# Hybrid SSD, attention and mixture-of-experts block: Silu and splits on VectorE, the expert pairs' steps in another order, the last pair in one piece, the final norm by tiles

## The chip, the cores and the metric

The kernel runs on one core of a Trainium2 chip. TensorE (PE, with its weight loads as PEld), VectorE (DVE), ScalarE (ACT) and GpSimd (POOL) work in parallel, each through its own instructions in order, and meet through semaphores; SyncE (SP) issues nearly all DMAs. The metric is device time in microseconds of one execution.

## The reference

One transformer layer over 256 tokens of width 1024, in fp32: a projection of the normed input to some 6,500 columns, a Mamba2 mixer (causal convolution over four taps, Silu, a scan over chunks), a sparse attention mixer, their gated sum, and a mixture of experts, here the part that the change touches most:

```
xbc = jax.nn.silu(xbc + conv_b)                      # after the convolution
yg = yg * lax.rsqrt(jnp.mean(yg * yg, axis=-1, keepdims=True) + NORM_EPS)   # per group of 512
...
for e in range(N_EXPERTS):                            # 32 experts, top 2 of 8 within one of 4 groups
    he = jax.nn.silu(t @ w_g[e]) * (t @ w_u[e])       # 1024 -> 256
    out = out + combine[:, e:e + 1] * (he @ w_d[e])   # 256 -> 1024
...
return _rmsnorm(h, final_g)
```

## The kernel before

**First part, to about 473 us.** Projections are computed from weights that stream through slots of 1 MB. Each fp32 operand is split into a high and a low part: `split` (L217) has ACT copy the high part to `wh` and another engine subtract it to give the low part `wl` (L231 on POOL for every fourth of a range of splits, otherwise on DVE through `tt`, L91). PE then does three products. The order of the instructions on each engine in this part is made by a scheduler from its own estimates of cost, so the source shows less than the order lists do. From 62 to 107 us PE projects queries and keys (`qk`), from 107 to 170 the rest of the convolution's input (`pj_xb`), and between these stand the convolution's taps (L498 and `stt`, L88), ACT's Tanh (L504) and `conv_silu` (two POOL products, L508 and L509), and the rotary work (`RQ`). From 170 to 300 follow `z` and the attention, from 300 to 403 the gates and the scan, whose four groups each square y on ACT (`y2`) and sum the squares over the group's partitions by matmuls with a matrix of ones (`ysq`), then the output projections to 455, and the router.

**Experts, 473 to 694 us, written in order by hand** (`manual_schedule`, after L1457). 16 pairs p0 to p15 of two experts. A pair's tokens are gathered by a matmul with a 0/1 matrix, `DT`, into XG (for two pairs at a time: an odd pair gathers for the next two, `more`), 64 places per expert pair, the first 64 rows for the usual case and the other 64 (`others`) for an expert with more than 32 tokens, under a branch. Banks B4 to B7 of PSUM are shared. The steps of class `Pair`:

- `where` and `placed`: transposes of the weighted matrix `DW` into B5; from it DVE makes `DT` and `hp`, and ACT the routing weight of each row (`ws`, L1574).
- `up`: 32 matmuls into B4, gate and up of both experts side by side, k by k. `act`: Tanh (ACT, L1608), two products per half (DVE) into hp. `turn`: transposes of hp (L1617), `turned`: DVE copy to hT (`rw`, L1620).
- `down`: matmuls into B6. `result`: B6 times the gate g2 (DVE), copy of the high part (ACT, L1641), low part (DVE) into Y; Yo is the same for the others. `scatter`: matmuls of DT with Y's two parts into four accumulators (`acc`) that hold the residual stream, done in the next pair behind its `up`.
- `release` gives a weight slot back; SP then issues the next load in `stream`: per pair g, u, g, u, d, d of 1 MB each, for the last pair in 2, 4 and 2 pieces. SP waits in order for a slot.
- `general` is a loop over experts with still more tokens, that does nothing here; its register `ra` is loaded at pair 15 (L1687).

**End.** At pair 15, up and down go expert by expert. Then the final gain FG is loaded from ACT's queue (L1795), ACT loads the table of Sqrt (L1796), and the norm squares the accumulators (ACT, one on DVE), takes one root for both tiles and scales (L1813 to L1820).

## Time and profile before

| | us |
|---|---|
| median of three runs (lowest, highest) | 714.25 (708.05, 716.08) |
| profiled execution | 716.01 |
| its span | 714.0 |
| PE, DVE, ACT, POOL busy | 644.5, 470.2, 319.1, 63.0 |
| mean granted clock of TensorE | 0.972 |

The span is what the profile shows from the first to the last event; the execution is 2.0 longer. Times in the rows are from the start of the span. An engine that is busy all through a stretch sets its length; where none is, the waits tell which one was late. Of the granted clock, 1.00 is 2.4 GHz and 0.50 is 1.2 GHz.

### The profile page before, as it was taken

What the parts mean: (1) busy time and instruction counts of PE and PEld (TensorE: products, weight loads), DVE (VectorE), ACT (ScalarE), POOL (GpSimd) and SP (SyncE); (2) the same over time, 40 slices, a digit from 0 to 9 for tenths busy, and PEclk for the clock granted to TensorE, in tenths of its full rate; (3) what the DMA queues carried; (4) which work ended last, traced back from release to release, by engine and by line L of the source; (5) the groups of instructions that cost most, each with busy time, mean ns of one, the idle gap of its engine ahead of it and who ended that gap; (6) DMA issues with size and microseconds to landing.
All of it is one profiled execution on the core that took longest, in us unless ns stands there. A gap on an engine that the chain in (4) does not pass through costs nothing. (4 is left out here: it accounts for less than half of the span.)

```text
span 714.0 us, 14367 instructions
## 1 busy us (share of the span) xinstructions
PE 644.5 (90%) x5712; PEld 505.7 (71%) x5713; DVE 470.2 (66%) x1122; ACT 319.1 (45%) x622; POOL 63.0 (9%) x98
## 2 busy tenths in 40 slices
PE   6999989698999999999999999978888898888863
PEld 5889879697768778888988998755454554554530
DVE  3556899995789878695987677475454444554524
ACT  4335865663377776446554445421231212322212
POOL 2001682433000000000000000000000000000000
PEclk8899999999999999999999999998999999999986
DMA  8997941459748767626559888349999999999902
GB/s 269 334 344 253 363 136 21 158 178 308 226 160 283 256 198 253 219 77 219 173 182 351 345 344 315 122 162 380 375 421 419 419 419 421 418 420 417 371 12 89
DMA packets 102916, 193.28 MB, mean 271 GB/s; under 512 B 7716, under 2 KB 84020, under 8 KB 91316
## 3 DMA queue, kind: packets, MB, share of 16 engines
q1 hardware_dynamic: 101700, 190.26, 74.0%
q10 hardware_dynamic: 1136, 1.89, 0.9%
q8 instruction: 57, 0.93, 0.5%
q14 instruction: 23, 0.19, 0.1%
HBM read 190.98 MB, written 1.16 MB: 269 GB/s over the span
## 5 line engine op out<-in xcount | busy, mean ns | idle before, releaser
L105 PE MATMUL moe<-g,XG 128*32 128x256 f32 (+1 forms) x560 | 74.3, 385 | 3.5 <-PEq L1589 2.0
L105 PE MATMUL moe<-u,XG 128*32 128x256 f32 (+1 forms) x560 | 74.3, 386 | 0.0
L105 PEld LDWEIGHTS moe<-g,XG 128*32 128x32 f32 (+1 forms) x560 | 41.4, 113 | 39.0 <-issue 19.6
L105 PE MATMUL moe<-d,rw 128*32 128x512 f32 (+1 forms) x280 | 39.3, 644 | 15.2 <-ACT XG L1505 10.6
L88 DVE SCALAR_TENSOR_TENSOR hp<-hp,moe 64x256 f32<-64x256 f32 x32 | 13.4, 419 | 59.3 <-ACT hp L1608 59.1
L1608 ACT ACTIVATE hp<-moe 64x256 f32<-64x256 f32 x32 | 12.1, 378 | 65.1 <-PEq L1589 45.0
L105 PE MATMUL pj_z<-HH,wh 128*128 128x256 f32 x128 | 36.6, 286 | 2.6 <-DVE BC L88 2.1
L1574 ACT ACTIVATE moe<-moe 64x256 f32<-64x256 f32 x32 | 11.4, 356 | 59.3 <-DVE hp L95 58.8
L105 PEld LDWEIGHTS moe<-u,XG 128*32 128x32 f32 (+1 forms) x560 | 36.8, 113 | 0.0
L105 PE MATMUL pj_z<-HH,wl 128*128 128x256 f32 x128 | 36.8, 288 | 0.0
L105 PE MATMUL pj_z<-HL,wh 128*128 128x256 f32 x128 | 36.1, 282 | 0.0
L105 PE MATMUL moe<-DT,HFh 128*128 128x256 f32 x128 | 30.7, 291 | 2.1 <-DVE DT L91 1.1
L105 PEld LDWEIGHTS moe<-d,rw 128*32 128x32 f32 (+1 forms) x280 | 8.5, 117 | 33.8 <-issue 15.2
L919 ACT ACTIVATE P<-P,mn 128x128 f32<-128x128 f32 (+1 forms) x64 | 28.5, 448 | 6.4 <-DVE mn L916 5.4
L105 PE MATMUL pj_xb<-HH,wh 128*128 128x256 f32 x96 | 27.0, 282 | 3.9 <-DVE XSb L88 3.9
L105 PE MATMUL moe<-DT,HFl 128*128 128x256 f32 x128 | 29.6, 282 | 0.2 <-DVE HFl L88 0.2
L105 PE MATMUL moe<-Y,DT 64*128 64x512 f32 x128 | 20.7, 433 | 8.7 <-PEq L1589 3.3
L105 PE MATMUL xa<-HH,wh 128*128 128x256 f32 x96 | 28.6, 300 | 0.0
L91 DVE TENSOR_TENSOR moe<-moe,DW 128x512 f32<-128x512 f32 x16 | 11.2, 700 | 25.6 <-PE moe L105 13.1
L105 PE MATMUL pj_xb<-HH,wl 128*128 128x256 f32 x96 | 27.0, 281 | 0.9 <-DVE wl L91 0.9
L105 PEld LDWEIGHTS pj_z<-HH,wh 128*128 128x128 f32 x128 | 24.1, 188 | 5.3 <-issue 3.8
L91 DVE TENSOR_TENSOR wl<-so,wh 128x1024 fp32r<-128x1024 f32 x16 | 19.5, 1223 | 11.9 <-PE pj_so L105 10.8
(474 smaller groups left out, 2092.8 us busy)
## 6 DMA issues: line engine op xcount, KB each, us to landing
g<-in_w_exp_gate_dram SPq DMA_DIRECT2D x30, 1024.0 KB
u<-in_w_exp_up_dram SPq DMA_DIRECT2D x30, 1024.0 KB, 11.4
d<-in_w_exp_down_dram SPq DMA_DIRECT2D x30, 1024.0 KB, 16.8
ad<-in_w_ada_dram SPq DMA_DIRECT2D x16, 1024.0 KB, 6.3
ada<-in_w_ada_dram SPq DMA_DIRECT2D x16, 512.0 KB, 7.9
z<-in_w_in_dram SPq DMA_DIRECT2D x8, 1024.0 KB, 6.7
so<-in_w_ssm_out_dram SPq DMA_DIRECT2D x8, 1024.0 KB
qk<-in_w_in_dram SPq DMA_DIRECT2D x8, 936.0 KB, 7.3
```

Source lines behind the costliest of these rows:

```text
L88: return V.scalar_tensor_tensor(o, a, s, b, op0=op0, op1=op1)
L91: return V.tensor_tensor(o, a, b, op=op)
L105: return PE.matmul(o, l, r, start=start, stop=stop)
L919: A.activation(o, o, AF.Exp, bias=mn[:, n:n + 1], scale=-1.0, accum_out=sm[:, n:n + 1])
L1574: A.activation(B5[h, s * 256:(s + 1) * 256], B5[h, s * 256:(s + 1) * 256], AF.Copy, accum_out=self.ws[h])
L1608: A.activation(th[g], B4[g, s * 256:(s + 1) * 256], AF.Tanh, scale=0.5)
```

## The change

- All splits subtract on DVE; `conv_silu` is one DVE operation, q (tn + 1), in place of two POOL products.
- The four squares tiles of a group are added on DVE (two additions), and one matmul sums over the partitions in place of four.
- For pair 0 the routing arithmetic that needs no gather goes ahead of the gather on DVE, ACT makes all eight pieces of XG, and `where` goes between k = 5 and k = 6 of `up`.
- Odd pairs with a gather behind them: the second half of the gather and its copies come ahead of the next pair's `placed`.
- All other pairs: the first 64 rows are activated, turned into B7 and copied alone (`turn_of`, `turned_of`), then down; the other rows are turned behind down, and `placed` and the 0/1 matrices come behind that.
- The last pair's weights come as g, g, u, u, d, d in two pieces each; it does up and down in one; pair 14's scatter is behind its up; FG is loaded from SP after pair 14; the Sqrt table is loaded before down; `ra` is loaded after pair 13; the last scatter multiplies fp32 by halves of 256 columns straight from B6 times g2 (`scatter_last`).
- The norm goes tile by tile: accumulator times gain first, root of each tile apart, then the scaling.

Core of the diff:

```
-    for e in (NE - 2, NE - 1):
-        stream.append((f"g{e}", ld_rows(w_exp_gate, e, 2)))
-        stream.append((f"u{e}", ld_rows(w_exp_up, e, 4)))
-        stream.append((f"d{e}", ld_rows(w_exp_down, e, 2)))
+    for n, w in (("g", w_exp_gate), ("u", w_exp_up), ("d", w_exp_down)):
+        for e in (NE - 2, NE - 1):
+            stream.append((f"{n}{e}", ld_rows(w, e, 2)))
...
-        if PS0 <= st["split"] < PS1 and st["split"] % PSN == PSR:
-            G.tensor_tensor(lv, src, hv.bitcast(F32), op=OP.subtract)
-        else:
-            tt(lv, src, hv.bitcast(F32), OP.subtract)
+        tt(lv, src, hv.bitcast(F32), OP.subtract)
...
-        G.tensor_tensor(tn, tn, q, op=OP.mult)
-        G.tensor_tensor(q, tn, q, op=OP.add)
+        stt(q, tn, 1.0, q, OP.add, OP.mult)
...
+            tt(y2[0], y2[0], y2[1], OP.add)
+            tt(y2[0][:, 0:256], y2[0][:, 0:256], y2[0][:, 256:512], OP.add)
+            yield
             yb = ps(4, f"ysq{g}")[32 * g:32 * g + 32, 0:256]
-            for jj in range(2):
-                for j in range(2):
-                    mm(yb, ones[:, 0:32], y2[jj][:, j * 256:(j + 1) * 256], jj == 0 and j == 0, jj == 1 and j == 1)
+            mm(yb, ones[:, 0:32], y2[0][:, 0:256], True, True)
             A.activation(rs[32 * g:32 * g + 32], yb, AF.Copy)
...
+    def xg_copy(c, bank, first=False):
         for j in range(2):
             k, o, b_ = 2 * c + j, XG[:, (2 * c + j) * 256:(2 * c + j + 1) * 256], bank[:, j * 256:(j + 1) * 256]
-            if c % 2:
+            if c % 2 and not first:
...
-    for l in range(2):
-        for c, bank in enumerate((B4, B5, B6, B7)):
-            gather(bank, named, c, 256, (l,))
-            if l:
-                xg_copy(c, bank)
-    release("XK")
-    code = const([128, 16], "code", I32)
-    stt(code, ch, 2.0, qv[:, :, 0], OP.mult, OP.add)
     gs_ = rt(2)
     oh1, oh2, m1, m2, e2 = rt(2, 8), rt(2, 8), rt(2), rt(2), rt(2)
     ts(oh1, rank, 0.0, OP.is_equal)
     V.tensor_reduce(m1, leg, axis=AX.X, op=OP.max)
     stt(leg, oh1, -BIG, leg, OP.mult, OP.add)
     V.tensor_reduce(m2, leg, axis=AX.X, op=OP.max)
+    tt(e2, m2, m1, OP.subtract)
     ts(oh2, rank, 1.0, OP.is_equal)
-    tt(e2, m2, m1, OP.subtract)
+    V.tensor_reduce(gs_, ge, axis=AX.X, op=OP.add)
+    for l in range(2):
+        for c, bank in enumerate((B4, B5, B6, B7)):
+            gather(bank, named, c, 256, (l,))
     A.activation(e2, e2, AF.Exp)
-    V.tensor_reduce(gs_, ge, axis=AX.X, op=OP.add)
+    for c, bank in enumerate((B4, B5, B6, B7)):
+        xg_copy(c, bank, True)
+    release("XK")
+    code = const([128, 16], "code", I32)
+    stt(code, ch, 2.0, qv[:, :, 0], OP.mult, OP.add)
...
+        def act(self, parts=(0, 1)):
 
             lo, hi = slice(0, 64), slice(64, 128)
-            for s, (g, u) in enumerate(((lo, hi), (hi, lo))):
-                A.activation(th[g], B4[g, s * 256:(s + 1) * 256], AF.Tanh, scale=0.5)
-            for s, (g, u) in enumerate(((lo, hi), (hi, lo))):
+            gu = ((lo, hi), (hi, lo))
+            if 0 in parts:
+                for s, (g, u) in enumerate(gu):
+                    A.activation(th[g], B4[g, s * 256:(s + 1) * 256], AF.Tanh, scale=0.5)
+            for s in parts:
+                g, u = gu[s]
                 b = B4[:, s * 256:(s + 1) * 256]
                 stt(hp[u], th[g], 1.0, b[g], OP.add, OP.mult)
...
+        def turn_of(self, s):
+
+            q = slice(64 - 64 * s, 128 - 64 * s)
+            for m in range(2):
+                PE.transpose(B7[:, s * 128 + m * 64:s * 128 + (m + 1) * 64], hp[q, m:256:2], ident[q, q])
+
+        def turned_of(self, s):
+            V.tensor_copy(hT[:, :, 64 - 64 * s:128 - 64 * s],
+                          B7[:, s * 128:(s + 1) * 128].rearrange("p (m r) -> p m r", m=2))
+
...
+        def scatter_last(self):
+            mark(f"x_scatter{self.p}")
+            for n in range(2):
+                tt(YT[:, n], B6[:, n * 256:(n + 1) * 256], g2[:, n * 256:(n + 1) * 256], OP.mult)
+            for n in range(2):
+                for i in range(2):
+                    for hh in range(2):
+                        q = slice(64 * hh, 64 * hh + 64)
+                        mm(acc[i, hh][:, n * 256:(n + 1) * 256], self.DT[0][q, i * 128:(i + 1) * 128], YT[q, n], False, n == 1)
 
...
         if p == 15:
-            general()
-        if p < 15:
+            general(ra)
+        if p:
             P.up()
         else:
-            for j in range(2):
-                P.up((j,))
+            P.up(range(6))
+            P.where()
+            P.up(range(6, 8))
         P.asked()
         P.up_others()
         if not p:
-            P.where()
             P.placed()
-        if p < 15:
-            release(*(f"{n}{e}" for e in P.es for n in "gu"))
-        P.act()
+        release(*(f"{n}{e}" for e in P.es for n in "gu"))
         if more:
+            P.act()
             weighted(P.q + 1)
-        if prev and p < 15:
             prev.scatter()
             prev.scatter_others()
-        if more:
             for c, bank in enumerate((B6, B7)):
                 gather(bank, named, c, 256)
                 xg_copy(c, bank)
-        if nxt:
             nxt.where()
-        P.turn()
-        P.turned()
-        if nxt:
+            P.turn()
+            P.turned()
+            for c, bank in enumerate((B6, B7), 2):
+                gather(bank, named, c, 256)
+                xg_copy(c, bank)
             nxt.placed()
-        if not P.a and P.q < 7:
-            onehots(P.q + 1)
+        else:
+            P.act((0,))
+            if prev:
+                prev.scatter()
+                prev.scatter_others()
+            if nxt:
+                nxt.where((0,))
+            P.turn_of(0)
+            P.turned_of(0)
+            if nxt:
+                nxt.where((1,))
+            P.act((1,))
+        if p == 15:
+            A.activation(wss[0][0:1, 0:1], th[64:65, 0:1], AF.Sqrt, scale=0.0, bias=epsc[0:1])
+        P.down()
+        if not more:
+            P.turn_of(1)
+            P.turned_of(1)
+            if nxt:
+                nxt.placed()
+            if not P.a and P.q < 7:
+                onehots(P.q + 1)
+        P.down_others()
+        release(*(f"d{e}" for e in P.es))
+        if p < 15:
+            P.result()
+            P.result_others()
         if not p:
             left()
             release("G1")
-        if more:
-            for c, bank in enumerate((B6, B7), 2):
-                gather(bank, named, c, 256)
-                xg_copy(c, bank)
-        if p < 15:
-            P.down()
-            P.down_others()
-            release(*(f"d{e}" for e in P.es))
-            P.result()
-            P.result_others()
-        else:
-            P.down_others()
-            P.result_others()
-            for j in range(2):
-                P.down((j,))
-            P.result()
+        if p == 13:
+            ra = nc.values_load(any_[0:1, 0:1], min_val=0, max_val=4)
         if p == 14:
-            P.scatter()
-            P.scatter_others()
-    FG = slot("FG")
-    A.dma_start(FG[:, 0:1024], dram(final_g, 0, [[0, 128], [1, 1024]]))
-    A.activation(wss[0][0:1, 0:1], hp[32:33, 0:1], AF.Sqrt, scale=0.0, bias=epsc[0:1])
-    pairs[15].scatter_others()
-    pairs[15].scatter()
+            FG = slot("FG")
+            SP.dma_start(FG[:, 0:1024], dram(final_g, 0, [[0, 128], [1, 1024]]))
+    P.result_others()
+    P.scatter_others()
+    P.scatter_last()
 
 
     mark("last")
     OU, SJ = slot("OU"), slot("SJ")
     OUv, SJv = (t.rearrange("p (t d) -> p t d", t=2) for t in (OU, SJ))
-    sf, vf, rf = carve(rw_[:, 256:264], (2, 2), (2,), (2,))
-    for i in range(2):
+    sf, vf, rf, rv, r_ = carve(rw_[:, 256:268], (2, 2), (2,), (2,), (2,), (2,))
+
+    def cs(h):
+        return slice(h * 512, (h + 1) * 512)
+
...
+    half_norm(0)
+    times_g(0, 1)
+    times_g(0, 0)
+    root(0)
+    half_norm(1)
+    times_g(1, 1)
+    newton(0)
+    times_g(1, 0)
+    root(1)
+    for h in range(2):
+        ts(OUv[:, 0, cs(h)], OUv[:, 0, cs(h)], rf[:, 0:1], OP.mult)
+    SP.dma_start(out[0, 0:128, :], OUv[:, 0])
+    newton(1)
+    A.activation(OUv[:, 1, cs(1)], OUv[:, 1, cs(1)], AF.Copy, scale=rf[:, 1:2])
+    ts(OUv[:, 1, cs(0)], OUv[:, 1, cs(0)], rf[:, 1:2], OP.mult)
+    SP.dma_start(out[0, 128:256, cs(0)], OUv[:, 1, cs(0)])
+    A.dma_start(out[0, 128:256, cs(1)], OUv[:, 1, cs(1)])
```

DVE's list in an odd pair that gathers (pair 1): DW is the weighted 0/1 matrix, `XG<-moe,GC` the copies of gathered rows, `rw<-moe` the copy of the turned activations, `DT<-moe` and `hp<-moe` are `placed`. Before:

```order
L91 TENSOR_TENSOR DW<-DT,comb 128x2x64
L91 TENSOR_TENSOR DW<-DT,cE 128x2x64
L96 TENSOR_SCALAR XG<-moe_5299,GC 128x256 x2
L1620 COPY rw<-moe_5296 128x256
L95 TENSOR_SCALAR DT<-moe_5297 128x256
L95 TENSOR_SCALAR hp<-moe_5297 128x256
L96 TENSOR_SCALAR XG<-moe_5299,GC 128x256 x2
L1589 UNCONDITIONAL_BRANCH
L91 TENSOR_TENSOR moe_5298<-moe_5298,DW 128x512
```

And now:

```order
L90 TENSOR_TENSOR DW<-DT,comb 128x2x64
L90 TENSOR_TENSOR DW<-DT,cE 128x2x64
L95 TENSOR_SCALAR XG<-moe_5283,GC 128x256 x2
L1618 COPY rw<-moe_5280 128x256
L95 TENSOR_SCALAR XG<-moe_5283,GC 128x256 x2
L94 TENSOR_SCALAR DT<-moe_5281 128x256
L94 TENSOR_SCALAR hp<-moe_5281 128x256
L1584 UNCONDITIONAL_BRANCH
L90 TENSOR_TENSOR moe_5282<-moe_5282,DW 128x512
```

The second pair of XG copies moved ahead of `placed`; on ACT its own XG copies moved the same way ahead of the sums of `ws`.

PE's list of pair 0, from the end of `up`'s branch to pair 1's first matmul: `DW` rows are `where`, `hp` rows the turns, the rows that end in `,rw 32x512` down. Before (the 16 are pair 0's own eight and pair 1's eight):

```order
L1589 UNCONDITIONAL_BRANCH
L105 MATMUL moe_5297<-ident,DW 64x128 x16
L1617 MATMUL moe_5296<-ident,hp 128x128 x2
L105 MATMUL moe_5298<-d_4716,rw 32x512 x2
L105 MATMUL moe_5298<-d_4718,rw 32x512 x2
L105 MATMUL moe_5298<-d_4716,rw 32x512 x2
L105 MATMUL moe_5298<-d_4718,rw 32x512 x2
```

And now, behind an `up` that already has pair 0's own eight `where` rows in it:

```order
L1584 UNCONDITIONAL_BRANCH
L104 MATMUL moe_5281<-ident,DW 64x128 x4
L1624 MATMUL moe_5283<-ident,hp 128x64 x2
L104 MATMUL moe_5281<-ident,DW 64x128 x4
L104 MATMUL moe_5282<-d_4700,rw 32x512 x2
L104 MATMUL moe_5282<-d_4702,rw 32x512 x2
L104 MATMUL moe_5282<-d_4700,rw 32x512 x2
L104 MATMUL moe_5282<-d_4702,rw 32x512 x2
L1624 MATMUL moe_5283<-ident,hp 128x64 x2
```

The turn is split in two, the first ahead of half of the next pair's `where`, the second behind down; pair 0's own `where` has left this place.

PE's end. `Y,DT` and `Yo,DT` rows are the last scatter, into the four accumulators; the branch above them ends the others' scatter. Before:

```order
L1656 UNCONDITIONAL_BRANCH x2
L105 MATMUL moe_5292<-Y,DT 128x512
L105 MATMUL moe_5293<-Y,DT 128x512
L105 MATMUL moe_5292<-Y,DT 128x512
L105 MATMUL moe_5293<-Y,DT 128x512
L105 MATMUL moe_5294<-Y,DT 128x512
L105 MATMUL moe_5295<-Y,DT 128x512
L105 MATMUL moe_5294<-Y,DT 128x512
L105 MATMUL moe_5295<-Y,DT 128x512
```

And now:

```order
L1674 UNCONDITIONAL_BRANCH x2
L104 MATMUL moe_5276<-Yo,DT 128x256
L104 MATMUL moe_5277<-Yo,DT 128x256
L104 MATMUL moe_5278<-Yo,DT 128x256
L104 MATMUL moe_5279<-Yo,DT 128x256
L104 MATMUL moe_5276<-Yo,DT 128x256
L104 MATMUL moe_5277<-Yo,DT 128x256
L104 MATMUL moe_5278<-Yo,DT 128x256
L104 MATMUL moe_5279<-Yo,DT 128x256
```

The scatter is eight matmuls of 256 columns from one fp32 tile in place of eight of 512 from Y's two parts, the accumulators' left halves first.

## Rows read from the trace of the kernel before

**Rows 1.** The page, its part 1 (busy time, share of the span and instructions of each engine) and of part 2 the mean busy share of the core's 16 DMA engines in forty equal slices of 17.85 us, in tenths.

```profile
PE 644.5 (90%) x5712; PEld 505.7 (71%) x5713; DVE 470.2 (66%) x1122; ACT 319.1 (45%) x622; POOL 63.0 (9%) x98
...
DMA  8997941459748767626559888349999999999902
```

**Rows 2.** The windows view by stage: from and to, length, then busy time and number of instructions of PE, PEld, DVE, ACT and POOL, the granted clock, the DMA share and GB/s. The stages are the projection of queries and keys, the second half of the convolution with the rotary work beside it, the scan, and the experts' loop from the second pair's loads on.

```profile
62.00:107.00 45.00, 42.50 (x216) 36.67 (x215) 38.59 (x68) 34.46 (x49) 30.98 (x18) 1.00 0.84 275
107.00:170.00 63.00, 53.68 (x445) 50.29 (x443) 57.49 (x86) 38.20 (x64) 23.51 (x14) 1.00 0.45 142
300.00:403.00 103.00, 103.00 (x865) 92.64 (x865) 83.48 (x153) 55.26 (x70) 0.16 (x2) 1.00 0.63 215
478.00:680.00 202.00, 173.48 (x1898) 106.06 (x1902) 99.70 (x249) 50.27 (x134) 0.00 (x0) 0.97 0.99 402
```

**Rows 3.** The waits view of PE from 62 to 172 us: the waiting group, what it waited for, us in total, times, the longest.

```profile
PE pj_xb L105 <- DVE XSb L88: 3.9, 2, 3.2
PE qkp L105 <- POOL wl L231: 2.4, 2, 1.8
```

**Rows 4.** The timeline of DVE: start, duration of all instructions of the row, engine, line, operation, out<-in, shapes, count, and in brackets the idle time before with what ended it.

```profile
70.83 1.13 DVE L91 TENSOR_TENSOR wl<-qk,wh 128x936 fp32r<-128x936 f32 x1
...
82.88 1.92 DVE L91 TENSOR_TENSOR wl<-qk,wh 128x936 fp32r<-128x936 f32 x1
...
110.73 0.68 DVE L91 TENSOR_TENSOR RQ<-RQ 128x512 f32<-128x512 f32 x1
```

**Rows 5.** The timeline of POOL, same columns.

```profile
83.89 2.07 POOL L509 TENSOR_TENSOR XSa<-cv,XSa 128x512 f32<-128x512 f32 x1
```

**Rows 6.** DVE's groups of one shape from 62 to 175 us: line, operation, out<-in, shape, count, then busy us in total, mean ns of one, and idle time before.

```profile
L91 DVE TENSOR_TENSOR wl<-qk,wh 128x936 fp32r<-128x936 f32 x12 | 18.0, 1514 | 5.9 <-ACT wh L229 5.9
...
L91 DVE TENSOR_TENSOR RQ<-QKV,cs 128x512 f32<-128x512 f32 x8 | 9.7, 1232 | 0.1
L91 DVE TENSOR_TENSOR wl<-z,wh 128x1024 fp32r<-128x1024 f32 x4 | 6.7, 1671 | 1.8 <-ACT wh L229 1.8
```

**Rows 7.** POOL's groups in the same stretch, same columns.

```profile
L231 POOL TENSOR_TENSOR wl<-qk,wh 128x936 fp32r<-128x936 f32 x4 | 8.8, 2200 | 63.7 <-ACT wh L229 63.7
L231 POOL TENSOR_TENSOR wl<-xb,wh 128x1024 fp32r<-128x1024 f32 x3 | 7.8, 2607 | 15.6 <-ACT wh L229 15.6
```

**Rows 8.** The timeline of PE in the scan, the row of one group's sum of squares.

```profile
304.59 1.91 PE L105 MATMUL ysq<-y,ones 128*32 128x256 f32 x8
```

**Rows 9.** The timeline of all engines in pair 0: the transposes that place its weights (`where`), the tanh, the down projection, pair 1's first up matmul.

```profile
478.38 1.28 PE L105 MATMUL moe<-ident,DW 128*64 128x128 f32 x16 [1.14 <-DVE DW L91]
...
481.63 0.75 ACT L1608 ACTIVATE hp<-moe 64x256 f32<-64x256 f32 x2
...
485.57 3.64 PE L105 MATMUL moe<-d,rw 128*32 128x512 f32 x16 [0.52 <-DVE rw L1620]
...
489.39 0.41 PE L105 MATMUL moe<-g,XG 128*32 128x256 f32 x2 [0.18 <-PEq L1589]
```

**Rows 10.** The timeline from the end of pair 9 to the start of pair 11: pair 9's down projection, pair 10's first up matmul, the scatter of pair 9's result, the turn, pair 10's down projection, pair 11's first up matmul.

```profile
619.92 1.92 PE L105 MATMUL moe<-d,rw 128*32 128x512 f32 x16 [1.47 <-ACT XG L1505]
...
622.02 0.41 PE L105 MATMUL moe<-g,XG 128*32 128x256 f32 x2 [0.18 <-PEq L1589]
...
626.39 1.20 PE L105 MATMUL moe<-Y,DT 64*128 64x512 f32 x8 [0.71 <-PEq L1589]
...
629.11 0.50 PE L1617 MATMUL moe<-ident,hp 128*128 128x128 f32 x2 [0.27 <-DVE hp L88]
...
630.13 1.92 PE L105 MATMUL moe<-d,rw 128*32 128x512 f32 x16 [0.52 <-DVE rw L1620]
...
632.23 0.41 PE L105 MATMUL moe<-g,XG 128*32 128x256 f32 x2 [0.18 <-PEq L1589]
```

**Rows 11.** The waits view over the whole span, one line.

```profile
PE moe L105 <- ACT XG L1505: 10.6, 7, 1.8
```

**Rows 12.** The windows view along the stream of expert weights, columns as in group 2.

```profile
488.00:492.00 4.00, 3.82 (x57) 1.93 (x53) 2.95 (x9) 0.60 (x1) 0.00 (x0) 0.85 0.71 272
508.00:512.00 4.00, 4.00 (x68) 1.98 (x64) 1.29 (x2) 0.28 (x1) 0.00 (x0) 1.00 0.71 256
640.00:660.00 20.00, 17.05 (x220) 10.35 (x216) 10.57 (x24) 5.09 (x14) 0.00 (x0) 1.00 1.01 418
668.00:670.00 2.00, 1.14 (x12) 0.42 (x16) 0.42 (x1) 0.80 (x2) 0.00 (x0) 1.00 0.98 319
678.00:680.00 2.00, 1.48 (x14) 0.54 (x18) 1.09 (x3) 0.43 (x2) 0.00 (x0) 1.00 0.27 109
686.00:688.00 2.00, 2.00 (x14) 0.92 (x12) 0.00 (x0) 0.00 (x0) 0.00 (x0) 0.50 0.00 0
```

**Rows 13.** The timeline of the last pair: its first up matmul, the tanh, the down projection, the start of the norm, the last scalings.

```profile
685.43 0.61 PE L105 MATMUL moe<-g,XG 128*32 128x256 f32 x1 [1.51 <-PEq L1687]
...
694.40 0.77 ACT L1608 ACTIVATE hp<-moe 64x256 f32<-64x256 f32 x2 [12.24 <-PEq L1589]
...
698.26 3.17 PE L105 MATMUL moe<-d,rw 128*32 128x512 f32 x16 [0.52 <-DVE rw L1620]
...
704.29 0.69 DVE L1809 COPY SJ<-moe 128x512 f32<-128x512 f32 x1 [0.63 <-PE moe L105]
...
707.88 2.72 DVE L88 SCALAR_TENSOR_TENSOR OU<-moe,rw,FG 128x512 f32<-128x512 f32 x4
```

More of the change, by code (lines that the diff above doesn't have):

```diff
@@ L34 @@
 WARM3 = 12
-PS0, PS1, PSN, PSR = 17, 44, 4, 1
 RATE_XB, RATE_ATTN, RATE_SSD = 1.15, 1.5, 1.35
@@ L1558, in __init__, with where @@
             self.DT, self.ws, self.last = DTs[p % 2], wss[p % 2], p == 15
-        def where(self):
+        def where(self, ss=(0, 1)):
             mark(f"x_where{self.p}")
-            for s in range(2):
+            for s in ss:
                 for i in range(2):
```

55 lines of the change are left out of this document (26 added, 29 removed).

## The prediction

> **What bounds the kernel now.** I read the page first. PE is busy for 644.5 of the 714.0 us, DVE for 470.2, POOL for 63.0, and the DMA slices stand at 9 from the 28th on [rows 1]. An average says little here, so I went on by stages [rows 2]. The profiled execution took 716.0 us (span 714.0 and 2.0 around it); that is 1.8 above the median 714.25 of three runs that lie 8 us apart. The sum is made against 716.0.
>
> Three stages matter. From 62 to 170 us PE idles 2.5 + 9.3 = 11.8 us (length less busy), while DVE is busy 38.6 of 45 and 57.5 of 63 [rows 2]; PE's longest waits there are for DVE (3.9) and for a POOL subtraction (2.4) [rows 3]. From 300 to 403 PE has no idle time at all: 103.0 of 103 [rows 2]. In the expert loop PE is busy 173.5 of 202 and the DMA share is 0.99 [rows 2], so two chains run side by side: PE with the engines that feed it, and the weight stream. The stream is done in the window 678 to 680 (share 0.27, so about 678.5) [rows 12], but pair 15 starts only at 685.43 [rows 13]. From the last byte to the end of the span pass 35.5 us in which nothing is loaded for the experts.
>
> **The change, part by part.**
>
> *Splits and Silu to DVE.* POOL loses 7 subtractions (means 2.20 and 2.61) [rows 7] and 24 Silu products; the one on the timeline took 2.07 [rows 5]. DVE gains 7 subtractions at 1.13 alone [rows 4], the 1024-wide ones at 1024/936 of that: 4 x 1.13 + 3 x 1.24 = 8.2 us; and 12 fused products over 128x512 from SBUF, for which the nearest row is 0.68 [rows 4]: 8.2. Together +16.4. Against it: DVE's own operations with two SBUF inputs are longer beside POOL. The subtraction at 82.88 took 1.92 with POOL at work, that at 70.83 took 1.13 [rows 4, 5]; the means are 1.51, 1.23 and 1.67 where alone they are 1.13, 0.68 and about 1.24 [rows 4, 6]. With the counts 12, 8 and 4 that is 4.6 + 4.4 + 1.7 = 10.7 us in these three groups; with the small groups I estimate 18. Net on DVE: about -2. PE gains more than that, since the wait for POOL (2.4) goes and Silu is no longer two POOL steps behind the taps. Bounds: -11.8 (all PE idle time) and +16.4 (no relief, all on the path). I take **-5**, near the wait for POOL plus the net relief, because most of the idle time also hangs on the order that the scheduler lays out anew.
>
> *Sum of squares.* Each of four groups has 8 records in 1.91 us on a PE without idle time [rows 8, 2]; two stay. 4 x 1.3 = 5.2 us go. DVE pays 0.68 + about 0.4 per group, in a stage where it is busy 83.5 of 103 [rows 2]; if it were late, PE would wait. Bounds 0 and -5.2; I take **-5**, for the matmul has other work queued before it.
>
> *First pair.* DVE's routing arithmetic is taken out of the way of the gather's results and ACT makes all XG pieces, so DW is ready before the up projection ends. Before: `where` at 478.38, tanh at 481.63, down at 485.57, pair 1 at 489.39, and down took 3.64 instead of 1.92 because the clock stood at half after the idle stretch [rows 9, 10]. By the same steps, tanh comes at about 479.7 and pair 1 at about 486.4: -3.0. Worst case 0: ACT's pace of 0.5 per k against up's 0.46 may hold up the projection.
>
> *Odd pairs.* The second gather and its copies now stand ahead of `placed`. PE waited 10.6 us in 7 pairs for the copy into XG before down, 1.47 of it at pair 9 [rows 10, 11]; ACT then has nothing between. 7 x 1.35 = -9.5 (bounds 0, -10.6).
>
> *Even pairs.* From the start of the scatter to the start of down pass 3.74 us (626.39 to 630.13) [rows 10]; with the first rows turned alone, down waits for two DVE operations less, about 0.9, at 0.25 more PE work after down: 7 x (0.85 - 0.25) = -4.2. The result comes later, but the next up (3.7) covers it.
>
> *Last pair.* Between pair 14's down and pair 15's up stand a wait for Y, the scatter and the 1.51 of a register load [rows 13]: 4.5 us that go behind the up or to pair 13. PE alone would start pair 15 at 685.4 - 3.0 - 9.5 - 4.2 - 4.5 = about 664.
>
> *The weight stream.* That is before the weights. The stream ends at 678.5; its holes at 488 and 508 (share 0.71 of 4 us each: 2.3 us) [rows 12] go with the earlier releases, larger pieces at the end bring back about 1.0 (319 GB/s against 418) [rows 12], pair 0's release is later by 0.6: 675.8. The two down tiles are the last 5.0 us of it (1.05 MB at 418 GB/s each), so u31's first half is there at about 669.3. **PE waits about 5 us, and the stream becomes the bound.** Before, PE's idle stretch ahead of pair 15 left the clock at half (0.50 at 686 to 688, the 1.2 GHz level) [rows 12], so I price pair 15's up between 3.7 at full and 6.9 at half clock, at 6: 675.3. Tanh, products, half turn and copy 2.65 (today 698.26 - 694.40 = 3.86 [rows 13] less 0.9 and less the 0.3 of a shorter copy): 678. Down 3 (today 3.17): 681. Result times gate and fp32 scatter without Y: 2.4. Norm: today 9.7 from 704.29 to the end [rows 13]; of which the four scalings are 2.72; by tiles I count 9.9, four multiplications and four scalings in place of the four, overlapped with the squares, so no gain. End at 692.9 in the time of before: **-21.1** for experts and end together (bounds -28, if the clock holds and the stream ends a pair's piece earlier, and -14, if up and down run at half clock throughout and the holes stay).
>
> **Sum:** 716.0 - 5 - 5 - 21.1 = 684.9. I predict **685**. I don't take off the 1.8 to the median, as the three runs spread by more.
>
> **The page against the rows.** Pair 0's down, after idle time, took 3.64 against 1.92, and pair 15's up ran at 0.50 [rows 9, 10, 12]. The Trainium skill ("TensorE: Matmul & The Clock Gate", section "HAM oscillation — how this bites in real kernels") says that a kernel whose matmuls are shorter than its wait for weights has every tile start at the throttled clock. That speaks against a change which makes PE faster than its stream; it would give about 692 in place of 685. Rows show it only after the two long idle stretches, and in between the granted clock is 1.00 [rows 2, 12].
>
> **Rivals.**
>
> 1. *The front gives nothing.* DVE stays at its limit from 62 to 170 since the added 16.4 eats the relief, and the sum of squares waits for DVE. For it: DVE at 57.5 of 63 [rows 2]. Against: the stretch beside POOL is measured. Time: 685 + 5 + 5 = 695.
> 2. *More of the front, warm end.* All idle time of 62 to 170 goes (-11.8 in place of -5) and pair 15 runs at full clock (-2.3 on up): 676. For it: PE's work from 62 on is dense; against: pair 15 must wait for weights.
> 3. *Half clock whenever PE has caught up.* PE is 20 us faster than now in a loop whose stream gives only 3 us, so the difference appears as waits from pair to pair, not only at pair 15; pairs that start after one run slow, and the last pair's up, down and scatter all do: +3.2 + 1.7 + 1.9 against warm ones, that is +3 to +4 on the forecast, and as much again in earlier pairs: 692.
> 4. *The pairs don't do what they should.* The half turn exposes the DVE (Y later than the next scatter, the tanh of pair 2n+1 behind `placed` on ACT), and even pairs gain nothing; then PE reaches pair 15 at about 668 and hardly waits. The stream hides this: 685 to 688; it is inside the forecast.
> 5. *Slower.* In the front, DVE works in order: a Silu product waits for ACT's Tanh and holds back the taps and subtractions behind it, on which PE waits. With 24 POOL steps gone, DVE has 16.4 us more, and if no operation gets shorter (something else than POOL stretches them) and each of the 12 products waits for a Tanh (0.75 for pair 0's two [rows 9]) and the two copies out of PSUM before it (about half a us each, my estimate), 1.7 in all, the front costs 16.4 + 20 = 36 in place of -5: 726. It decides from 26 us on, where the end's 21 and the scan's 5 are used up. Against: 18 of 108 us of DVE's time are stretch, and POOL's rows coincide with it [rows 4, 5].
>
> **How the numbers follow.** A measurement of this kernel tells 1% (7 us) from no change. Forecast with rival 4, 678 to 692: 0.47. Rival 1 (690 to 699): 0.23. Rival 2 (670 to 679): 0.14. Rival 3 (688 to 697): 0.09. Rival 5: 0.03; something between 700 and 721, half of rival 5 or the end's gain halved: 0.04. The range of 675 to 699 leaves out half of rival 2, the last two and a bit of each edge: about 0.18. Faster by over 1% is below 707: 0.47 + 0.23 + 0.14 + 0.09 = 0.93; within 1%: 0.04; slower: 0.03.
>
> **What would show it.** Right: no wait of PE for POOL at 62 to 170, and DVE's 936-wide subtraction near 1.13 in the mean; the ysq row with 2 records; pair 1's up some 3 us after where it would stand by shorter first stages; no PE wait for XG; PE waiting for a DMA at pair 15's up, at a clock below 1.00, with the stream's last byte some 17 us before the end instead of 35.5. Wrong: DVE's busy time from 62 to 170 over 105 us of 108 with PE waiting for it (rivals 1, 5); DVE's subtractions still at 1.5 without POOL; PE's clock below 1.00 in pairs 8 to 14 (rival 3); or pair 15 starting without a wait for weights (the loop gained less than I count).

## The result, and the profile after

The changed kernel takes 689.67 us in the median of four runs (688.08 to 693.53), the kernel before 712.85 beside it; the ratio is 0.969 with an interval of 0.962 to 0.976. A second set (experiment 9) gave 690.99 and 0.970 (0.967 to 0.974). The profiled execution took 688.08 with a span of 686.3, 27.7 less than before. It is the fastest of its set, and that of the kernel before (716.01) nearly the slowest, so 27.7 is more than the 23.2 between the medians. 685 was forecast, with 675 to 699 around it. Single executions of one kernel lie up to 8 us apart, and the first matmul of the query projection alone starts anywhere from 63.5 to 67.2 us; parts are therefore read as distances within one trace. The profiled execution of the first experiment (698.16) was a slow one, at a lower clock; it is left out of that experiment's time, and only the waits around pair 15 are read from it.

The page of the changed kernel, parts 1 and 2, answers to [rows 1]:

```profile
PE 637.4 (93%) x5714; PEld 503.2 (73%) x5715; DVE 467.8 (68%) x1160; ACT 323.9 (47%) x629; POOL 8.1 (1%) x67
...
DMA  8997970578657758636477998637999999999971
```

POOL has given up 55 us. The DMA engines are full from the 29th slice on, which begins at 480 us (before: from the 28th, at 482), and the last expert weights landed at 666.94, 19.4 us before the end (before: at 680.50, 33.5 before it). The windows view of the first stages and of the scan, columns as in [rows 2]:

```profile
62.00:107.00 45.00, 44.03 (x221) 38.79 (x220) 40.64 (x79) 34.94 (x50) 0.96 (x1) 1.00 0.85 275
107.00:170.00 63.00, 59.21 (x518) 53.91 (x517) 54.29 (x100) 39.73 (x68) 0.00 (x0) 1.00 0.58 186
300.00:403.00 103.00, 102.58 (x878) 94.61 (x878) 84.57 (x141) 55.59 (x68) 1.73 (x6) 1.00 0.68 239
```

PE's idle time from 62 to 170 fell from 11.8 to 4.8 us, though DVE's busy time only went from 96.1 to 94.9. The scan has PE full as before. DVE's groups from 62 to 175 us, to be held against [rows 6]:

```profile
L90 DVE TENSOR_TENSOR wl<-qk,wh 128x936 fp32r<-128x936 f32 x16 | 18.1, 1130 | 3.0 <-ACT wh L227 3.0
...
L90 DVE TENSOR_TENSOR RQ<-QKV,cs 128x512 f32<-128x512 f32 x8 | 5.4, 681 | 0.0
...
L87 DVE SCALAR_TENSOR_TENSOR XSb<-pj_xb,T,XSb 128x255 f32<-128x255 f32 x4 | 1.9, 472 | 0.0
```

The subtraction is back at the 1.13 that it took alone, the rotary product went from 1.23 to 0.68, and the tap, which reads one operand from PSUM, kept its 0.47. The sum of squares, once four matmuls [rows 8], in PE's timeline:

```profile
299.57 0.62 PE L104 MATMUL ysq<-y,ones 128*32 128x256 f32 x2
```

Pair 0 in the timeline of all engines (`where`, tanh, down, pair 1's up), to be held against [rows 9]:

```profile
464.23 1.09 PE L104 MATMUL moe<-ident,DW 128*64 128x128 f32 x16
...
467.37 0.75 ACT L1605 ACTIVATE hp<-moe 64x256 f32<-64x256 f32 x2
...
470.11 3.58 PE L104 MATMUL moe<-d,rw 128*32 128x512 f32 x16
...
474.23 0.41 PE L104 MATMUL moe<-g,XG 128*32 128x256 f32 x2
```

From the start of `where` to pair 1's up pass 10.0 us in place of 11.0, and `where` itself comes ahead of the end of up. PE's waits over the whole span, to be held against [rows 11]:

```profile
PE moe L104 <- DVEq L1704: 4.2, 1, 4.2
...
PE moe L104 <- ACT XG L1500: 1.2, 7, 0.2
```

The wait for XG went from 10.6 to 1.2, and a wait for DVE's queue stands in the list. Where it is, the timeline from pair 14's last result to the norm shows, to be held against [rows 13]:

```profile
659.68 0.68 DVE L90 TENSOR_TENSOR Yo<-moe,DW 128x512 f32<-128x512 f32 x1
...
660.48 0.41 PE L104 MATMUL moe<-g,XG 128*32 128x256 f32 x2 [4.19 <-DVEq L1704]
...
665.98 0.77 ACT L1605 ACTIVATE hp<-moe 64x256 f32<-64x256 f32 x2 [6.94 <-PEq L1584]
...
668.61 1.92 PE L104 MATMUL moe<-d,rw 128*32 128x512 f32 x16 [0.38 <-DVE rw L1627]
...
672.22 2.00 PE L104 MATMUL moe<-Yo,DT 64*128 64x256 f32 x16 [1.31 <-DVE Yo L90]
673.82 0.60 ACT L1836 ACTIVATE SJ<-moe 128x512 f32<-128x512 f32 x1 [5.46 <-PE moe L104]
...
675.24 1.29 DVE L90 TENSOR_TENSOR OU<-moe,FG 128x512 f32<-128x512 f32 x2 [2.74 <-ACT SJ L1836]
```

PE stood idle for 4.19 us and began pair 15 0.12 after DVE had finished pair 14's last product (659.68 + 0.68). The windows view of that place:

```profile
656.00:658.00 2.00, 0.29 (x2) 0.15 (x2) 1.56 (x4) 0.56 (x3) 0.00 (x0) 1.00 1.02 406
658.00:660.00 2.00, 0.00 (x0) 0.00 (x0) 0.92 (x2) 1.03 (x3) 0.00 (x0) 1.00 1.03 410
660.00:662.00 2.00, 1.52 (x24) 0.86 (x28) 0.36 (x1) 0.00 (x0) 0.00 (x0) 0.81 1.01 389
662.00:664.00 2.00, 2.00 (x24) 0.99 (x20) 0.00 (x0) 0.00 (x0) 0.00 (x0) 0.50 0.66 246
```

The weights were still streaming at 410 GB/s while PE idled, and the clock, 1.00 throughout that idle time, fell to 0.50 within the up. By the DMA semaphores in the trace the last up tile (u31) landed in two halves at 659.90 and 661.19: the first was there 0.6 us before PE began.

In distances, before and after, with the forecast's share; the last column is the profiled execution of the same changed kernel in experiment 9:

| stretch | before | after | change | forecast | after, again |
|---|---|---|---|---|---|
| start to first query matmul | 66.9 | 65.6 | -1.3 | 0 | 65.1 |
| to the gate projection | 215.4 | 209.6 | -5.8 | -5 | 209.7 |
| gate projection to the expert part | 174.2 | 169.1 | -5.1 | -5 | 169.3 |
| to pair 1's up | 33.0 | 29.9 | -3.1 | -3 | 29.9 |
| pair 1's up to pair 14's | 181.6 | 170.8 | -10.8 | -13.1 | 174.4 |
| pair 14's up to pair 15's | 14.5 | 15.5 | +1.0 | 0 | 15.3 |
| pair 15's up to the end | 28.6 | 25.8 | -2.7 | -5 | 25.8 |

All stretches repeat within some half a microsecond except the one from pair 1 to pair 14: 10.8 less in one execution, 7.2 in the other.

(The forecast of pair 15's up was 212.9 us after the start of the expert part, held by the weights; it came after 216.2.)

### The profile page after: what moved, and what is told of

The parts are those of the page before. It is cut to its first block, busy times and chain, and to the rows that moved or that the text cites. A ratio compares the mean times of both kernels' runs of the same rounds, so it can differ in the third digit from the quotient of the medians.

```text
span 686.3 us, 14364 instructions
## 1 busy us (share of the span) xinstructions
PE 637.4 (93%) x5714; PEld 503.2 (73%) x5715; DVE 467.8 (68%) x1160; ACT 323.9 (47%) x629; POOL 8.1 (1%) x67
## 3 DMA queue, kind: packets, MB, share of 16 engines
HBM read 190.98 MB, written 1.16 MB: 280 GB/s over the span
## 5 line engine op out<-in xcount | busy, mean ns | idle before, releaser
L104 PE MATMUL moe<-g,XG 128*32 128x256 f32 (+1 forms) x560 | 71.2, 388 | 6.4 <-DVEq L1704 4.2
L104 PE MATMUL moe<-u,XG 128*32 128x256 f32 (+1 forms) x560 | 71.6, 388 | 0.0
L104 PEld LDWEIGHTS moe<-g,XG 128*32 128x32 f32 (+1 forms) x560 | 39.3, 114 | 33.5 <-issue 12.2
L1569 ACT ACTIVATE moe<-moe 64x256 f32<-64x256 f32 x32 | 11.4, 356 | 66.0 <-DVE hp L94 65.5
L1500 ACT ACTIVATE XG<-moe,GC 128x256 f32<-128x256 f32 x36 | 18.1, 565 | 32.4 <-PE moe L104 32.4
L104 PEld LDWEIGHTS moe<-DT,HFh 128*128 128x128 f32 x128 | 23.2, 189 | 5.6 <-issue 5.6
L104 PE MATMUL xa<-HL,wh 128*128 128x256 f32 x96 | 27.0, 284 | 0.0
L104 PE MATMUL pj_xb<-HL,wh 128*128 128x256 f32 x96 | 26.8, 279 | 0.0
L104 PE MATMUL xa<-HH,wl 128*128 128x256 f32 x96 | 26.3, 282 | 0.0
```

Of the source, the lines that this page charges most:

```text
L104: return PE.matmul(o, l, r, start=start, stop=stop)
L1500: A.activation(o, b_, AF.Identity, scale=GC[:, 1, k:k + 1], bias=GC[:, 0, k:k + 1])
L1569: A.activation(B5[h, s * 256:(s + 1) * 256], B5[h, s * 256:(s + 1) * 256], AF.Copy, accum_out=self.ws[h])
```

## The experiments

All are edits of the changed kernel; times are medians.

**1. The join ahead of pair 15.** Pair 15's first up matmul writes bank B4. In the loop for still more tokens DVE and ACT read B4, so that matmul waits until DVE has passed the loop's branch, which stands in DVE's list behind pair 14's results. In the loop, everywhere:

```
-B4
+B7
```

> The changed kernel, with one edit: in the loop for still more tokens (which has no turn here) bank B4 is replaced by B7, so that no later writer of B4 has to wait until VectorE has passed that loop's branch. In the changed kernel PE stands idle 4.19 us ahead of pair 15's up and starts it at 660.48, 0.12 after VectorE ends pair 14's last result. Theory join (the wait is for VectorE, in whose list the branch stands behind pair 14's three results): the wait falls under 1.5 us, up starts at about 657.5 and takes 3.7 to 4.5 us in place of 5.33 because the clock does not fall; the span shrinks by 3 to 5 us. Theory weights (rival, that of the prediction: the last up tile lands only then): the wait stays at 4 us, the trace names a DMA, and the span stays within 1 us of 686.3.

687.9 in the median of four executions (685.03 to 692.07), 1.8 below the changed kernel. The timeline of this kernel around pair 15 (first up matmul, DVE's last product for pair 14, the scatter, down):

```profile
667.23 0.41 PE L104 MATMUL moe<-g,XG 128*32 128x256 f32 x2 [1.57 <-PEq L1704]
...
669.06 0.68 DVE L90 TENSOR_TENSOR Yo<-moe,DW 128x512 f32<-128x512 f32 x1
...
672.92 1.59 PE L104 MATMUL moe<-Y,DT 64*128 64x512 f32 x8 [2.03 <-PEq L1584]
...
675.58 3.64 PE L104 MATMUL moe<-d,rw 128*32 128x512 f32 x16 [0.39 <-DVE rw L1627]
```

Up starts before DVE is through, and 1.57 us is left of the 4.19: the join was the wait. The time did not follow by 3 to 5 us. What PE meets next, the last up tile, experiment 8 shows. The 3.64 of down is not read as a reason, for with the same edit it took 1.92 and 1.96 in experiments 8 and 9. Theory join holds for the wait and falls for the gain.

**2. The norm of before.**

```
-    half_norm(0)
-    times_g(0, 1)
...
+    rsqrt(rf, vf, 2, "rf")
...
```

> The changed kernel with the norm of the kernel before (one root for both tiles, one square on VectorE, scaling straight from the accumulators); all else as changed. In the changed kernel the end of the last scatter to the end of the span takes 12.1 us (674.22 to 686.3), in the kernel before 9.0 (704.96 to 714.0). Theory norm (the norm by tiles is slower by itself, since VectorE's multiplications wait for ScalarE's squares of the same accumulator): scatter's end to the end of the span is 9 to 9.5 here, the span 683 to 684. Rival (the scatter in halves, the position of the table load or the cold clock make the end longer): it stays at 11.5 or more.

Scatter's end to the end of the span took 8.8 us (678.01 to 686.8), so the norm by tiles costs 3.3 more. 688.52: at the level of the time little of it is seen. In the profiled execution pairs 3 and 4 were slower (pair 1's up to pair 14's up 174.5), with the clock at 0.50 for part of each.

**3. The norm in another order.**

```
-    half_norm(0)
     times_g(0, 1)
+    square(0, 0)
+    square(0, 1)
     times_g(0, 0)
...
+    A.activation(OUv[:, 0, cs(1)], OUv[:, 0, cs(1)], AF.Copy, scale=rf[:, 0:1])
...
```

> The changed kernel with the norm by tiles in another program order: each product with the gain that meets an accumulator whose square is to come later is written ahead of that square, and ScalarE scales half of tile 0. Theory norm, as a matter of order (whoever is written second waits for the other engine's read of the same accumulator): VectorE's first product starts beside ScalarE's first square, the second tile's squares start 1.5 us earlier, and scatter's end to the end of the span falls from 12.1 to 9.3 to 10.3. Rival (the wait has another cause, such as the gain's DMA): the first product still starts 1.4 us after the first square and nothing is won.

9.5 us (676.14 to 685.65). The first product now starts 0.04 behind the first square (675.77 and 675.73) and not 1.42. The order it is: in this program, of two engines that read one accumulator, the one that is written second waits for the first. The edit also gives ACT one of tile 0's two scalings, and what each of the two is worth was not taken apart. 689.73 in all, again with slower pairs (173.0).

**4. Splits and Silu back on GpSimd.**

```
-        tt(lv, src, hv.bitcast(F32), OP.subtract)
+        if PS0 <= st["split"] < PS1 and st["split"] % PSN == PSR:
+            G.tensor_tensor(lv, src, hv.bitcast(F32), op=OP.subtract)
...
```

> The changed kernel with every fourth split of the middle range and both Silu products back on GpSimd; all else as changed. The z projection of the changed kernel starts at 153.13 us, that of the kernel before at 162.66. Theory relief (VectorE's subtractions and rotary products are drawn out by GpSimd, and that costs PE the waits): z starts 7 to 9.5 us later than in the changed kernel, VectorE's 936-wide subtractions go back from 1.13 to about 1.5 us in the mean, the time rises by 6 to 9 us. Rival (the gain of the first stages comes from the other edits or from the new order by the scheduler): z starts within 3 us of 153.

695.91, +6.2. From the first query matmul to the z projection pass 97.2 us; 87.5 in the changed kernel, 95.8 before. DVE's group in this kernel:

```profile
L91 DVE TENSOR_TENSOR wl<-qk,wh 128x936 fp32r<-128x936 f32 x12 | 18.1, 1514 | 6.5 <-ACT wh L228 6.4
```

Theory relief holds for splits and Silu together; they were not undone one by one. The Trainium skill ("SBUF — State Buffer", section "SBUF: two separate sides") says that of a VectorE operation with two SBUF inputs and a GpSimd operation that reads SBUF the one that starts second blocks. Under "Who interferes with whom" it says that VectorE operations with at most one SBUF input, outside its two-port modes, do not contend. The trace agrees: 1514 against 1130 ns here, and 0.47 for the taps with and without GpSimd.

**5. Four matmuls for the sum of squares.**

```
-            tt(y2[0], y2[0], y2[1], OP.add)
...
-            mm(yb, ones[:, 0:32], y2[0][:, 0:256], True, True)
+            for jj in range(2):
+                for j in range(2):
...
```

> The changed kernel with the sum of squares as before: four matmuls per group, no additions on VectorE. From the first matmul of the gate projection (pj_gs) to the first of the ssm output projection (pj_so) the kernel before took 100.9 us, the changed one 93.2; from pj_gs to the expert part 174.2 and 169.1. Theory matmuls (PE has no idle time there, so the records removed are the gain): the first stretch takes 97.5 to 99.5, the second 173.5 to 175, the time rises by 4 to 6 us. Rival (the gain of that stage comes from work that the scheduler moved to another stage): the second stretch stays within 1.5 us of 169.1.

Gate projection to the ssm output projection: 100.7 (97.5 to 99.5 expected); to the expert part 174.0, 4.9 more than in the changed kernel. Theory matmuls holds for the stage; the time, 692.16, rose by only 2.5, within the spread of single executions. In its profiled execution pair 0's down ran at full clock (1.92 in place of 3.58).

**6. Odd pairs as before.**

```
+            nxt.placed()
             for c, bank in enumerate((B6, B7), 2):
...
-            nxt.placed()
```

> The changed kernel with the second half of the odd pairs' gather and its copies back behind the next pair's placing. Theory: PE's wait for the copies into XG goes from 1.2 us back to about 10 in seven pairs, the odd pairs without a stall behind up go from 12.9 to 14.2 or more, and pair 1's up to pair 14's up takes 179 to 181 us in place of 170.75; all of it reaches the end: the time rises by 8 to 10 us. Rival (the stream of weights bounds the loop and PE's gain there was hidden): the time rises by less than 4 us.

701.12, +11.4; pair 1's up to pair 14's up 182.0. Both are above what was expected. Six of the seven odd pairs took 1.3 to 1.6 more each, pair 3 took 2.9 more, with the clock at 0.50 from 509.7 to 513.1. PE's wait in this kernel:

```profile
PE moe L104 <- ACT XG L1500: 10.6, 7, 1.7
```

All of it reached the end, so PE's chain, not the stream, was the limit through the loop, though the DMA share is 1.01 in both.

**7. Whole turn in the even pairs.**

```
-            P.act((0,))
+            P.act()
...
-            P.turn_of(0)
-            P.turned_of(0)
+            P.turn()
+            P.turned()
...
```

> The changed kernel with a whole turn ahead of down in the even pairs and the last one, placing ahead of down, as before. Theory: even pairs take 0.5 to 0.8 us more each (pair 10 went from 10.21 to 9.48, pair 12 from 9.67 to 9.19), so pair 1's up to pair 14's up takes 3 to 4.5 us more than 170.75; in pair 15 the tanh to down takes 3.8 in place of 2.6; together the time rises by 4 to 6 us. Rival (the half turn only shifts VectorE's work and what it wins is lost behind down, where the second turn and the results come later): the time is the same within 1.5 us.

Pair 1's up to pair 14's up 174.8, +4.0, but little of this is the half turn. From the scatter to the next pair's up, pair 10 took 5.84 us (605.04 to 610.88), as in the kernel before [rows 10], and 5.36 in the changed kernel (603.20 to 608.56). Pair 12 lost the same 0.48, the pairs 2, 6 and 8 only 0.14 to 0.16, and pair 4 was 0.32 shorter: 1.1 in all six, against the 0.5 to 0.8 expected in each. The greater part stands elsewhere: 2.0 in pair 13 (a pause of 1.62, and the clock at 0.50 from 640.3 to 643.7) and 0.7 in pair 1, whose up began at 0.50. In pair 15 tanh to down took 3.76 (3.8 expected) in place of 2.63. But 691.62 in all, +1.9: the wait ahead of pair 15 was 2.83 in place of 4.19, since DVE had no second copy and no placing behind down. Part of what the half turn wins was given back there.

**8. Three edits at the end together:** the first, the third, and

```
         P.down()
+        if p == 15:
+            for n in range(2):
+                tt(YT[:, n], B6[:, n * 256:(n + 1) * 256], g2[:, n * 256:(n + 1) * 256], OP.mult)
...
```

> The changed kernel with three edits together: B7 in place of B4 in the loop for still more tokens (no join ahead of pair 15's up), the norm by tiles in the other program order, and the last pair's down result times the gate written right behind down, ahead of the second turn's copy and of the others' result. Theory: PE's idle time ahead of pair 15's up is under 1.6 us; the end of down to the end of the scatter takes 2.6 in place of 3.7; the scatter's end to the end of the span 9.6 in place of 12.1; the time is 682 to 685 where the clock stays up through the last pair, 685 to 688 where it falls after the up as it did in the profile of the run without the join. Rival (the parts at the end don't add up, since what is taken from one wait shows in the next): 687 or more.

686.69 in the median, and 684.29 in the profiled execution, where the clock stayed up (682 to 685 expected). Its timeline (pair 15's first up matmul; two later ones; the result times the gate; the norm's first square and first product):

```profile
658.13 0.41 PE L104 MATMUL moe<-g,XG 128*32 128x256 f32 x2 [1.54 <-PEq L1702]
...
660.45 0.40 PE L104 MATMUL moe<-u,XG 128*32 128x256 f32 x1 [1.69 <-SPq L1702]
...
663.33 0.40 PE L104 MATMUL moe<-u,XG 128*32 128x256 f32 x1 [0.94 <-SPq L1702]
...
669.99 0.75 DVE L90 TENSOR_TENSOR Yo<-moe,DW 128x256 f32<-128x256 f32 x2 [1.08 <-PE moe L104]
...
672.69 0.60 ACT L1855 ACTIVATE SJ<-moe 128x512 f32<-128x512 f32 x1 [4.95 <-PE moe L104]
672.74 1.49 DVE L90 TENSOR_TENSOR OU<-moe,FG 128x512 f32<-128x512 f32 x2 [1.20 <-PE moe L104]
```

With the join gone PE meets the next wait, 1.69 and 0.94 us inside up for SP's queue, which waits for the two halves of the last up tile; they landed at 660.41 and 663.28. The clock stays at 1.00 up to the scatter. Down's end to the scatter's end is 3.2 in place of 3.7 (the expected 2.6 missed: the scatter now waits for PE's own branch), and square and product start together.

**9. Changed kernel and that version once more, on one chip.**

> The changed kernel itself once more, beside the next three on one chip. Both theories below expect 687 to 691 and, from the first matmul of the expert part (the moe rows' start) to pair 15's first up matmul, 215 to 218 us.

> The version with the three edits at the end once more (B7 in place of B4 in the loop for still more tokens, the norm's other order, the result written right behind down). Theory: 2.5 to 4.5 us under the changed kernel on this chip: 2.5 from the norm, 1 from the result, 0 to 1.5 from the join, since PE there meets the last up tile next, 2.6 us of waits inside pair 15's up. Rival (the ends don't add up): within 1.5 us of it.

690.99 (688.89 to 695.28) and 684.22 (682.69 to 685.20); the version's ratio to the kernel before is 0.960 (0.957 to 0.962). In the changed kernel pair 15's up came 219.6 us after the start of the expert part, past the 215 to 218 expected. The version is 6.8 below it, more than the 2.5 to 4.5 expected; pair 1's up to pair 14's up was 174.4 in the one profile and 170.8 in the other, and the edits touch nothing ahead of pair 15. The 3.6 between them is TensorE's clock. PE's timeline of pairs 3 and 4 in the changed kernel's repeat (pair 3's scatter, the beginning of pair 4's down):

```profile
508.88 1.19 PE L104 MATMUL moe<-Y,DT 64*128 64x512 f32 x8 [2.33 <-issue]
...
527.69 2.79 PE L104 MATMUL moe<-d,rw 128*32 128x512 f32 x12
```

Behind the pause of 2.33 the clock stood at 0.50 from 510.5 to 513.9, and once more from 527.5 to 530.9, where pair 4's down took 3.51 in place of 1.92. Pair 3 took 16.8 and pair 4 12.3 us, against 15.3 and 10.3 in the first profile of the same kernel, which had the same pause of 2.33 and a clock of 1.00 behind it. So some 3 us of the 6.8 are left for the edits, as far as one profile of each can tell. The version beats both kernels.

**10. Without the last expert's gate and up loads** (its matmuls take expert 30's, so the output is another):

```
+            if n == "d" or e < NE - 1:
                 stream.append((f"{n}{e}", ld_rows(w, e, 2)))
```

> The version with the three edits, and in addition gate and up weights of the last expert are not loaded: its matmuls use those of expert 30, so the stream is 2.1 MB shorter (5.0 us at 418 GB/s) and PE does the same work. Theory stream (after the join is gone, pair 15 is held by the arrival of its last up tile, and the clock is not the issue): no PE wait for a load inside the up, which takes 3.7 in place of 6.7 us, and the time falls by 2.5 to 3.5 us against the version with all loads. Rival (PE's own chain sets pair 15, the waits inside the up are covered by something else, such as the scatter's Y): less than 1 us.

683.38, 0.8 less: theory stream fails at the time, though the waits for loads are gone and up takes 3.66. PE's timeline of pair 14 and of the start of pair 15 tells why:

```profile
650.66 0.49 PE L104 MATMUL moe<-Y,DT 64*128 64x512 f32 x2 [0.15 <-PEq L1585]
653.05 0.98 PE L104 MATMUL moe<-Y,DT 64*128 64x512 f32 x6 [1.90 <-DVE hp L87]
...
656.72 3.64 PE L104 MATMUL moe<-d,rw 128*32 128x512 f32 x16
...
661.73 0.41 PE L104 MATMUL moe<-g,XG 128*32 128x256 f32 x2 [0.94 <-PEq L1703]
```

Between the scatter's second and third matmul PE idled 1.90 us; behind that the clock was at 0.50 from 654.0 to 660.8, down took 3.64 in place of 1.92, and pair 15 started 2.3 later after pair 14's up than in the version of 9. In this execution the clock took what the stream gave; whether it does so in the others was not seen.

**11. The last pair's loads in the old order and pieces.**

```
-    for n, w in (("g", w_exp_gate), ("u", w_exp_up), ("d", w_exp_down)):
-        for e in (NE - 2, NE - 1):
-            stream.append((f"{n}{e}", ld_rows(w, e, 2)))
+    for e in (NE - 2, NE - 1):
+        stream.append((f"g{e}", ld_rows(w_exp_gate, e, 2)))
...
```

> The changed kernel with the last pair's weights in the order and pieces of the kernel before: gate in 2, up in 4, down in 2 pieces, expert by expert; all else as changed, up and down in one. Theory stream: u31 is now behind d30 and in smaller pieces, its last piece comes 2 to 3.5 us later than in the changed kernel, so the up ends 2 to 3.5 us later, and the time rises by as much. Rival (VectorE's results and the join set pair 15, not the weights): the up starts 4.2 us after the turn as in the changed kernel, and the time stays within 1 us.

692.83, 1.8 above the control on this chip, whose runs spread by 6: not settled by the time. The wait ahead of pair 15 was 4.19 to the hundredth, as in the changed kernel and in the experiments 2 to 6: it is DVE's chain that sets it, not the arrival of a tile. The last up tile did come later, as expected (219.6 us after the start of the expert part, 216.9 in the changed kernel), but PE came later still: pair 14's down ran at clock 0.50 (3.64) and pair 15 began at 220.8. So the order of the loads stays untried as a limit.

## Why the prediction was right, and where its steps were off

*Splits and Silu* (-5): -5.8. The mechanism is shown for the two together: no added time on DVE, because what was added equals what GpSimd had cost it. PE gained more up to the z projection (8.3) and lost 2.5 in the stage behind.

*Sum of squares* (-5): -5.1, shown by experiment 5. *First pair* (-3.0): -3.1, by the trace alone.

*Odd pairs* (-9.5): the wait went from 10.6 to 1.2, and undoing it cost 1.3 to 1.6 in each of six pairs. Right in kind and size.

*Even pairs* (-4.2): right in kind, mis-sized. The 0.6 was read at pair 10 and taken for seven pairs. From the scatter to the next up pairs 10 and 12 gained 0.48, pairs 2, 6 and 8 only 0.14 to 0.16. In pairs 2 and 8 the scatter of the others' rows (1.9 us of matmuls) stands between scatter and turn and had covered DVE's products before; in pair 6 the others' down waits for the second turn.

The 10.8 of pairs 1 to 14 is therefore in part luck. Pair 4 alone gained 2.65, some 2 of it because the kernel before had a pause of 1.94 there and the clock at 0.50 behind it. Against that, a pause between up and scatter grew in two odd pairs (0.47 to 2.33 us at pair 3, 0.48 to 1.16 at pair 13), for which the profile names PE's own sequencer or nothing. In experiment 4 pair 3 had it inside the scatter (1.74). Its cause was not tried. In the repeat the same pairs gained 7.2.

*Last pair.* Here the step that failed is "PE waits about 5 us, and the stream becomes the bound". PE waited 4.19, but for DVE. The sum had moved pair 14's scatter behind the up and the register load to pair 13, and left in place what the loop's branch makes PE wait for. So one of the prediction's own signs of being wrong appeared: pair 15 started without a wait for weights. The stream was close, though. The first half of the last up tile was there 0.6 us before PE began, in the repeat 4.2 before; with the join gone, up waited for this tile, 2.6 us in experiment 8 and 1.5 in 9. Pair 15 started 3.3 late against its count, and 2.7 of that is the stream's: this half landed 215.6 us after the start of the expert part, not 212.9. The count set out from an end of the stream at 678.5, by a window's share; in that trace the last piece landed at 680.50. And PE was ready at 656.3, 212 after the start, where the sum has about 208: that 4.19 is near the 5 is luck.

*The end.* Up 5.35 (priced 6), tanh to down 2.63 (2.65), down 1.92 (3), the scatter's end 3.69 behind down (2.4), the norm 12.5 from its first square (9.9). Two terms were mis-sized, by 3.9 together: "result times gate and fp32 scatter without Y: 2.4" left out that the second turn's copy and the others' result stand ahead of it on DVE; and the count of the norm overlapped products and squares that read the same accumulator, which the order does not allow. Up and down came out 1.7 shorter than priced, which hid part of it. The terms as they stand add up to 693.3 for the end, not 692.9.

*The whole.* The sum took 31.1 off an execution of 716.0, near the slowest of the kernel before; the medians lie 23.2 apart. Off the median of 712.85 it would have given 681.7, 8 below what was measured and still inside the range. So 685 owes some of its nearness to where it started from.

*Rivals.* DVE did not take over the front (1, 5). Rival 4 was right about pairs 2, 6 and 8. Rival 3 showed in part, and not in every execution. In the profile of the result the clock was at 1.00 through pairs 2 to 14, and at 0.50 in pair 15's up behind its idle time. In the repeat it also fell in pairs 3 and 4 and cost some 3.5 us; in experiments 2, 3, 5, 6, 7, 10 and 11 it fell somewhere in pairs 3 to 14, each time behind a pause of PE of 1.2 to 2.8 us. Pauses of 2.33 and 2.60 also stand in profiles where it stayed up (the result's and experiment 8's), so the pause alone does not decide it. The rule beside rival 3, that of the Trainium skill ("TensorE: Matmul & The Clock Gate", section "HAM oscillation — how this bites in real kernels"), has every tile start at the throttled clock. The trace does not show that: over the loop, from 470 to 650 us, the mean granted clock was 0.99.

## What to carry to other kernels

When an edit takes a step off the path, ask what the instruction behind it waits for by its operands: a loop that never runs still joins the engines that it names, through the banks it would use. An expected gain at the end of a chain is worth only the distance to the next wait, here 0.6 us from the last up tile's first half to VectorE's last result in one execution, and 4.2 in another; take the waits in turn, and read each in the trace before pricing the next. And moving work from GpSimd to VectorE can be free where the two were in each other's way.

## What the runs showed that I had not expected

Two things. The clock is the first: of one kernel, with the same pause of 2.33 us at pair 3, one profile has 1.00 behind it and another 0.50, and that makes 3.6 us of the time from pair 1 to pair 14 (experiment 9).

The second: the scatter in pair 14, one piece of 1.20 before, broke in two. (Before, that happened in pair 4, with 1.94 in the middle.) PE's timeline of it in the changed kernel:

```profile
649.37 0.50 PE L104 MATMUL moe<-Y,DT 64*128 64x512 f32 x2
651.32 0.96 PE L104 MATMUL moe<-Y,DT 64*128 64x512 f32 x6 [1.45 <-DVE hp L87]
```

The third matmul needs Y, done at 646.58, yet starts at 651.32, 0.23 after DVE's second product for pair 14's activations. The register load for all engines, which the change moved to the end of pair 13, suggests itself, but doesn't make the pause alone: with the load at the same place the scatter ran in one piece in experiment 5, and in experiment 7, where 1.63 us passed behind it instead; in the other profiles the pause was 0.8 to 1.9. Pauses of this size for which the trace names PE's sequencer or nothing also moved from pair to pair between the kernels. What they wait for was not tried and stays open.
